# Weight pieces that hold four K tiles of both column tiles, a turned last K tile, and banks by last use, in a two-layer hybrid transformer

## The chip, the cores and the metric

The kernel runs on one core of one Trainium2 chip. The metric is the device time of one execution in microseconds. The kernel before takes 2865.7 us, the median of three runs (2864.64 to 2867.15).

## The reference

Two layers act on x, 256 tokens of width 2048, in float32. Each layer is a feed-forward half step, a mixer, and another feed-forward half step; each begins with an RMS norm and adds to x.

```python
for layer in range(DEPTH):
    x = x + 0.5 * swiglu(rms_norm(x, ffn1_norm[layer]), w1_gate, w1_up, w1_down)
    h = rms_norm(x, mix_norm[layer])
    x = x + (delta_pool_mixer(h, ...) if layer % 2 == 0 else mla_mixer(h, positions, ...))
    x = x + 0.5 * swiglu(rms_norm(x, ffn2_norm[layer]), w2_gate, w2_up, w2_down)
```

`swiglu` is `(silu(h @ w_gate) * (h @ w_up)) @ w_down` with 4096 hidden columns. Layer 0's mixer is a gated delta rule of 8 heads (convolution, chunked triangular solve) joined with a pooling over four window widths. Layer 1's is latent attention of 16 heads: two low-rank projections of width 512 with norms, up-projections, head norms, rotary angles, causal softmax. Nearly all arithmetic is the multiplication of 256 tokens by weights that are read once from HBM, about 508 MB.

## The kernel before

**Precision in two parts.** Every float32 operand is held as a high part (a rounded copy in the fast float32 format) and a low part (the remainder). For weights, `split` (lines 170 to 172) makes them on the chip: ScalarE casts a raw weight tile to `whi` (line 171), VectorE subtracts to `wlo` (line 172). For activations `split_hi_lo` does the same (lines 152 to 162), and the two parts lie side by side in one tile of 2 x 256 columns.

**A step.** `step` (line 207) multiplies one K tile of 128 rows for a pair of column tiles, each with a PSUM bank of its own. Two matmuls with the high weights take both parts of the activation (512 columns), then two with the low weights take the high part (256 columns). All go through `mm` (line 205), so the profile shows one line for them; tile names tell them apart (`mm<-xg,whi`). The two halves of a bank are added when the bank is read (`joined`, lines 231 to 235, or `add_residual`, lines 351 to 357).

**Weights.** `paired_weights` (line 190) takes two column tiles at a time. It loads 2048 columns (16 K tiles) of each with one DMA of 1 MB on SP's queue, into one of three raw buffers, and splits them in pieces of 1024 columns: 8 K tiles of tile A, 8 of tile B, and so on. `whi` and `wlo` have four buffers each. `pair` (line 217) takes one piece of A and one of B for every eight steps. A piece lies at a small offset in its buffer of 1088 columns: A's high part at 16 and low part at 0, B's at 0 and 16. In the latent attention's up-projections (`both_sides`, line 180) one raw piece of 1024 columns holds four K tiles of both column tiles, and is split in two halves of 512 at offsets of its own, with two operations on each engine.

**Phases.** A feed-forward block (`ffn`, line 368) goes through 32 pairs of a gate and an up tile with 16 K tiles each, then (`project`, line 359) 8 pairs of output tiles with 32 K tiles. After each pair of the latter VectorE adds the two tiles into x (line 355), and the next norm's inputs are made at once: `feed_parts` (ScalarE line 159, VectorE line 160) multiplies x by the norm's gain and splits it, `feed_squares` (GpSimd lines 330 and 336, at the end ScalarE and VectorE) sums the squares. The norm's scale itself is applied late: the first pair of the next phase runs on unscaled activations, and `end_norm` (line 342) then puts one product with a matrix of ones behind that pair's last matmul, takes the reciprocal root, and hands out R, by which every result is multiplied. In the very first block the first two pairs (`opening`, line 374) are interleaved with the loading of x. The mixers go the same way: projections of pairs, work of their own, and `project`.

**PSUM.** Eight banks: `banks` (line 140) gives each phase a ring for the pairs ("mm") and one for all else ("aux"), 6 and 2 in the feed-forward blocks, 4 and 4 in the mixers. Each ring begins with its lowest bank in every phase.

**Order.** The code is written in the order of issue per engine. Side work of the mixers (norms of heads, attention of a head, the solve) runs as generators (`Chains`, line 56): a clock counts the estimated matmul time of what has been issued, and `poll` continues a generator once the clock has passed what it yielded. `LAG` is 1500 ns of that clock. In the latent attention `latent` (line 867) squares a low-rank tile on ScalarE, with the squares' remainder on GpSimd (line 248), yields 2 LAG, and then issues the product that sums the squares; `head_norm` (line 887) does so for each head, also with 2 LAG.

## Time and profile before

| | |
|---|---|
| median of three runs | 2865.7 us |
| the profiled execution | 2850.95 us, its span 2848.9 us |
| TensorE, weight loads busy | 2823.4 us (99%), 2456.5 us (86%) |
| VectorE, ScalarE, GpSimd busy | 1844.6 (65%), 1434.2 (50%), 192.7 us (7%) |
| read from HBM | 507.74 MB, 179 GB/s over the span |
| mean granted TensorE clock | 0.999 of full speed |

PE is TensorE's matmuls, PEld its weight loads, DVE is VectorE, ACT ScalarE, POOL GpSimd, SP the engine that issues the weights' DMAs. Matmuls are pipelined: the record of one is longer than the time until the next one starts, so starts and counts say how fast the stream goes, and a share of 99% doesn't. By its stages the execution goes: opening to 35 us, first feed-forward block to 539, mixer of layer 0 to 952 with the next norm's first pair, second block to 1480, layer 1's first block to 2007, latent attention to 2318, last block to 2849. A wait is listed by the engine and line that waited, and what ended it.

### The profile page before, as it was taken

Reading aid. Unit: us, or ns where it says so; the run is one execution under the profiler, and the core shown is the slowest. Engines: PE = TensorE matmul, PEld = TensorE weight load, DVE = VectorE, ACT = ScalarE, POOL = GpSimd, SP = SyncE. Lnnn points to the kernel's source line nnn. Section 1 sums busy time; section 2 is a strip of 40 time slices with the busy share of each in tenths; the row PEclk is TensorE's granted clock in tenths of the full one; section 3 lists DMA queues with packets and bytes.
Section 4 is the critical chain, followed back from the end, with each engine's and each line's share of the span. In section 5 each row is a group of like instructions: output and inputs, shape, how many; then the busy total and the mean of one; then the engine's idle time right before and its main releaser. Section 6 shows DMA issues by size and latency. Waiting matters only on the chain.

```text
span 2848.9 us, 41026 instructions
## 1 busy us (share of the span) xinstructions
PE 2823.4 (99%) x16378; PEld 2456.5 (86%) x16378; DVE 1844.6 (65%) x2789; ACT 1434.2 (50%) x2251; POOL 192.7 (7%) x239
## 2 busy tenths in 40 slices
PE   9999999999999999999999999999999999999999
PEld 8888888888988888888888888888888888888888
DVE  7666656677787666565556666666688766666544
ACT  6454543475564444444444545443588444445433
POOL 1000002000003000000110000011122210000000
PEclk9999999999999999999999999999999999999999
DMA  6555555545235545445555455555433354554554
GB/s 230 202 189 196 195 190 182 184 152 183 84 146 194 190 180 201 181 186 190 187 185 200 188 196 194 191 187 197 169 111 121 134 195 177 194 190 178 201 197 148
DMA packets 78528, 512.62 MB, mean 180 GB/s; under 512 B 10880, under 2 KB 14720, under 8 KB 17536
## 3 DMA queue, kind: packets, MB, share of 16 engines
q1 hardware_dynamic: 74736, 506.76, 48.3%
q10 hardware_dynamic: 3600, 3.25, 0.3%
q8 instruction: 128, 2.10, 0.3%
q14 instruction: 64, 0.52, 0.1%
HBM read 507.74 MB, written 2.10 MB: 179 GB/s over the span
## 4 chain that ended last, share of the span: by engine, by line
PE 92%; DVE 4%; issue 3%; POOL 1%; ACT 0%; DMA 0%; SPq 0%; DVEq 0%; POOLq 0%; ACTq 0%
PE mm L205 88%; PE aux L205 4%; DVE wlo L172 2%; POOL sq L248 1%; DVE xg L160 1%; DMA x<-in_x 0%; DVE y L486 0%; PE aux L642 0%; ACT whi L171 0%; DVE x L355 0%; PE aux L974 0%; DVE cb L767 0%; PE aux L682 0%; PE aux L345 0%; DVE z L234 0%
## 5 line engine op out<-in xcount | busy, mean ns | idle before, releaser
L172 DVE TENSOR_TENSOR wlo<-raw,whi 128x1024 fp32r<-128x1024 f32 (+1 forms) x982 | 1204.0, 1231 | 781.3 <-ACT whi L171 779.4
L205 PE MATMUL mm<-xg,whi 128*128 128x512 f32 x4880 | 1533.8, 394 | 4.8 <-DVE x L355 3.5
L171 ACT CAST whi<-raw 128x1024 fp32r<-128x1024 f32 (+1 forms) x982 | 1003.4, 1032 | 1031.5 <-PE mm L205 717.7
L205 PEld LDWEIGHTS mm<-xg,wlo 128*128 128x128 f32 x4880 | 917.1, 188 | 205.3 <-DVE wlo L172 6.2
L205 PE MATMUL mm<-xg,wlo 128*128 128x256 f32 x4880 | 973.9, 278 | 3.6 <-DVE wlo L172 3.5
L205 PEld LDWEIGHTS mm<-xg,whi 128*128 128x128 f32 x4880 | 745.8, 188 | 12.6 <-ACT whi L171 6.5
L205 PE MATMUL mm<-g,whi 128*128 128x512 f32 x2048 | 636.6, 392 | 0.0
L205 PEld LDWEIGHTS mm<-g,wlo 128*128 128x128 f32 x2048 | 384.5, 188 | 92.5 <-DVE wlo L172 7.5
L205 PE MATMUL mm<-g,wlo 128*128 128x256 f32 x2048 | 406.8, 278 | 2.0 <-DVE wlo L172 0.4
L205 PEld LDWEIGHTS mm<-g,whi 128*128 128x128 f32 x2048 | 309.8, 188 | 0.0
L156 ACT CAST g<-u 128x256 fp32r<-128x256 f32 x128 | 52.0, 406 | 166.4 <-DVE u L410 166.1
L135 ACT ACTIVATE t<-t 128x256 f32<-128x256 f32 x128 | 53.4, 417 | 100.0 <-DVE t L235 100.0
L157 DVE TENSOR_TENSOR g<-u,g 128x256 fp32r<-128x256 f32 x128 | 54.4, 425 | 57.5 <-ACT g L156 57.5
L330 POOL TENSOR_TENSOR acc<-x 128x256 f32<-128x256 f32 x6 | 3.7, 616 | 1193.8 <-DVE x L355 1146.6
L355 DVE SCALAR_TENSOR_TENSOR x<-mm,x 128x256 f32<-128x256 f32 x128 | 45.4, 417 | 57.9 <-PE mm L205 57.9
L330 POOL TENSOR_TENSOR sq<-x 128x256 f32<-128x256 f32 x70 | 54.0, 771 | 426.2 <-DVE x L355 332.7
L205 PE MATMUL mm<-o,whi 128*128 128x512 f32 x256 | 81.4, 395 | 0.0
L336 POOL TENSOR_TENSOR acc<-acc,sq 128x256 f32<-128x256 f32 x70 | 80.0, 1143 | 5.3
L234 DVE TENSOR_TENSOR t<-mm,t 128x256 f32<-128x256 f32 x177 | 72.7, 416 | 8.9 <-ACT t L233 8.6
L160 DVE SCALAR_TENSOR_TENSOR xg<-x,gains,xg 128x256 fp32r<-128x256 f32 x96 | 73.5, 802 | 5.1 <-ACT xg L159 5.1
L233 ACT COPY t<-mm 128x256 f32<-128x256 f32 x177 | 64.6, 372 | 8.4 <-PE mm L205 8.3
L205 PEld LDWEIGHTS mm<-o,wlo 128*128 128x128 f32 x256 | 47.9, 188 | 14.6 <-DVE wlo L172 5.5
(258 smaller groups left out, 1816.5 us busy)
## 6 DMA issues: line engine op xcount, KB each, us to landing
raw<-in_w1d SPq DMA_DIRECT2D x64, 1024.0 KB, 5.1
raw<-in_w2g SPq DMA_DIRECT2D x64, 1024.0 KB, 4.9
raw<-in_w2u SPq DMA_DIRECT2D x64, 1024.0 KB, 4.8
raw<-in_w2d SPq DMA_DIRECT2D x64, 1024.0 KB, 5.1
raw<-in_w1g SPq DMA_DIRECT2D x62, 1024.0 KB, 4.9
raw<-in_w1u SPq DMA_DIRECT2D x62, 1024.0 KB, 4.8
raw<-in_wqk SPq DMA_DIRECT2D x16, 1024.0 KB, 4.8
raw<-in_wgo SPq DMA_DIRECT2D x16, 1024.0 KB, 4.8
```

Source lines behind the costliest of these rows:

```text
L135: a = nc.scalar.activation(out, in_, func, **kw)
L156: nc.scalar.copy(dst[:, 0, :], src)
L157: nc.vector.tensor_tensor(dst[:, 1, :], src, dst[:, 0, :].bitcast(F32), op=ALU.subtract)
L160: nc.vector.scalar_tensor_tensor(dst[:, 1, :], src, scale, dst[:, 0, :].bitcast(F32), op0=ALU.mult, op1=ALU.subtract)
L171: self.last_cast = self.nc.scalar.copy(hi, src)
L172: self.nc.vector.tensor_tensor(lo, src, hi.bitcast(F32), op=ALU.subtract)
L205: return self.nc.tensor.matmul(out, lhsT, rhs, start=start, stop=stop)
L233: self.nc.scalar.copy(out, ps[:, S : 2 * S])
L234: self.nc.vector.tensor_tensor(out, ps[:, 0:S], out, op=ALU.add)
L330: eng.tensor_tensor(dst, self.x[d], self.x[d], op=ALU.mult)
L336: eng.tensor_tensor(self.acc, self.acc, dst, op=ALU.add)
L355: self.nc.vector.scalar_tensor_tensor(x, ps[:, c], 0.5, x, op0=ALU.mult, op1=ALU.add)
```

## The change

- `paired_weights` takes a list in which two column tiles have been interleaved on the host (`couples`): 512 columns (four K tiles) of one, then 512 of the other. One raw tile of 2048 columns then holds 8 K tiles of both. `both` splits 1024 columns with one operation per engine into both tiles' pieces of four K tiles, which lie 528 columns apart in the buffer. The second column tile comes first in a couple, so the high matmuls load from offset 528 and then from 0. The low matmuls of a step now go in reversed order, 0 and then 528.
- Gate and up, the down projections, both mixers' input and output projections and the up-projections use it. The latent attention's one unpaired input tile has a function of its own, `lone`. In the opening, each of the two loads of a block holds both tiles of one pair, not one tile of two pairs.
- Of the last K tile before a norm's product, the low matmuls come before the high ones (`turn`).
- `banks` sorts each ring by last use, longest unused first.
- In `latent` the wait before the squares' product is 4 LAG, not 2; in `head_norm` it is 3 LAG, not 2.

```diff
     def banks(self, mm, aux):
-        self.bank = {"mm": list(range(mm)), "aux": list(range(8 - aux, 8))}
+        recent = self.recent
+        self.bank = {"mm": sorted(range(mm), key=recent.index), "aux": sorted(range(8 - aux, 8), key=recent.index)}
     def psum(self, tag):
         q = self.bank[tag]
         q.append(q.pop(0))
+        self.recent.remove(q[-1])
+        self.recent.append(q[-1])
...
-    def both_sides(self, raw, h):
...
+    def couple(self, t):
+        return t[:, 0 : 2 * APART].rearrange("p (u c) -> p u c", u=2)[:, :, 0:512]
+    def both(self, raw, h):
+        hi, lo = (self.couple(t) for t in self.weight_tiles())
+        self.split(hi, lo, raw[:, h : h + 1024].rearrange("p (u c) -> p u c", u=2))
+        return [(hi[:, u, :], lo[:, u, :]) for u in (1, 0)]
     def paired_weights(self, slabs):
-        for u in range(0, len(slabs), 2):
-            two = slabs[u : u + 2]
-            for c in range(0, two[0].shape[1], 2048):
-                raws = [self.raw_tile() for _ in two]
-                for raw, ap in zip(raws, two):
-                    self.nc.sync.dma_start(raw, ap[:, c : c + 2048])
+        for ap in slabs:
+            for c in range(0, ap.shape[1], 2048):
+                raw = self.raw_tile()
+                self.nc.sync.dma_start(raw, ap[:, c : c + 2048])
                 for h in (0, 1024):
-                    yield [self.piece(raw, h, side) for raw, side in zip(raws, (SIDE_A, SIDE_B))]
+                    yield self.both(raw, h)
...
-    def step(self, ps, ws, act, first, last):
+    def step(self, ps, ws, act, first, last, turn=False):
         whole = act.rearrange("p a t -> p (a t)")
-        for o, (hi, lo) in zip(ps, ws):
-            self.mm(o, hi, whole, start=first, stop=False)
-        for o, (hi, lo) in zip(ps, ws):
-            self.last_mm = self.mm(o[:, 0:S], lo, act[:, 0, :], start=False, stop=last)
+        def high():
+            for o, (hi, lo) in zip(ps, ws):
+                self.last_mm = self.mm(o, hi, whole, start=first, stop=last and turn)
+        def low():
+            for o, (hi, lo) in list(zip(ps, ws))[::-1]:
+                self.last_mm = self.mm(o[:, 0:S], lo, act[:, 0, :], start=False, stop=last and not turn)
+        for f in ((low, high) if turn else (high, low)):
+            f()
...
-    def pair(self, stream, acts):
+    def pair(self, stream, acts, turn=False):
         K = len(acts)
-        ps = None
-        for k0 in range(0, K, 8):
-            pieces = next(stream)
-            ps = ps or [self.psum("mm") for _ in pieces]
-            for k in range(k0, k0 + 8):
-                c = slice((k - k0) * P, (k - k0 + 1) * P)
-                self.ch.wait(lambda: acts[k] is not None)
-                self.step(ps, [(hi[:, c], lo[:, c]) for hi, lo in pieces], acts[k], k == 0, k == K - 1)
-                self.ch.poll()
+        ps = [self.psum("mm") for _ in range(2)]
+        for k in range(K):
+            if k % 4 == 0:
+                pieces = next(stream)
+            c = slice(k % 4 * P, k % 4 * P + P)
+            self.ch.wait(lambda: acts[k] is not None)
+            last = k == K - 1
+            self.step(ps, [(hi[:, c], lo[:, c]) for hi, lo in pieces], acts[k], k == 0, last, turn and last)
+            self.ch.poll()
         return ps
...
             lat.setdefault(tag, []).append(o)
-            yield 2 * LAG
+            yield 4 * LAG
...
             b.squares(sq, t)
-            yield 2 * LAG
+            yield 3 * LAG
...
+def couples(u):
+    n, _, K = u.shape
+    return u.reshape(n // 2, 2, P, K // 512, 512)[:, ::-1].transpose(0, 2, 3, 1, 4).reshape(n // 2, P, 2 * K)
```

## Rows read from the trace of the kernel before

**Rows 1.** The page, busy time: engine, us, share of the span, instructions.
```profile
PE 2823.4 (99%) x16378; PEld 2456.5 (86%) x16378; DVE 1844.6 (65%) x2789; ACT 1434.2 (50%) x2251; POOL 192.7 (7%) x239
```
**Rows 2.** Windows, line 205: start:end, us, busy (matmuls), granted clock, DMA, GB/s.
```profile
1000.00:1100.00 100.00, 100.00 (x574) 87.09 (x573) 1.00 0.50 190
...
1600.00:1700.00 100.00, 100.00 (x591) 88.59 (x590) 1.00 0.49 190
```
**Rows 3.** Windows of three gate-and-up phases: PE, PEld, DVE, ACT, POOL busy (instructions).
```profile
952.00:1337.00 385.00, 385.00 (x2200) 335.42 (x2200) 237.89 (x341) 188.51 (x272) 2.96 (x3) 1.00 0.50 187
...
1480.00:1865.00 385.00, 385.00 (x2265) 340.90 (x2264) 243.93 (x349) 189.86 (x279) 2.97 (x3) 1.00 0.51 192
...
2318.00:2703.00 385.00, 385.00 (x2200) 335.46 (x2200) 235.81 (x339) 186.42 (x269) 0.00 (x0) 1.00 0.50 187
```
**Rows 4.** Timeline of PE at a pair start of a down projection: start, length.
```profile
431.56 0.62 PE L205 MATMUL mm<-g,whi 128*128 128x512 f32 x2
432.02 0.80 PE L205 MATMUL mm<-g,wlo 128*128 128x256 f32 x2
432.65 0.62 PE L205 MATMUL mm<-g,whi 128*128 128x512 f32 x2
```
**Rows 5.** Timeline of DVE just before the same pair start.
```profile
427.55 1.53 DVE L172 TENSOR_TENSOR wlo<-raw,whi 128x1024 fp32r<-128x1024 f32 x1
429.00 1.70 DVE L160 SCALAR_TENSOR_TENSOR xg<-x,gains,xg 128x256 fp32r<-128x256 f32 x2
430.62 1.75 DVE L172 TENSOR_TENSOR wlo<-raw,whi 128x1024 fp32r<-128x1024 f32 x1
```
**Rows 6.** Waits of PEld, four stretches in order: us in total, times, longest.
```profile
PEld mm L205 <- DVE wlo L172: 2.6, 6, 0.5
...
PEld mm L205 <- DVE wlo L172: 4.8, 12, 1.1
...
PEld mm L205 <- DVE wlo L172: 2.3, 6, 0.5
...
PEld mm L205 <- DVE wlo L172: 6.5, 13, 0.9
```
**Rows 7.** Groups by form, 2060 to 2200: busy us, mean ns, idle before.
```profile
L172 DVE TENSOR_TENSOR wlo<-raw,whi 128x512 fp32r<-128x512 f32 x40 | 30.1, 760 | 5.1 <-ACT whi L171 5.0
...
L172 DVE TENSOR_TENSOR wlo<-raw,whi 128x1024 fp32r<-128x1024 f32 x11 | 14.6, 1325 | 2.0 <-ACT whi L171 2.0
```
**Rows 8.** Waits of PE, whole execution: us in total, times, longest.
```profile
PE mm L205 <- DVE x L355: 3.5, 3, 1.2
```
**Rows 9.** Chain that ended last, around 1479 us: start, length, what.
```profile
1478.47 1.10 DVE x L355 x3
...
1479.71 3.48 PE mm L205 x18
```
**Rows 10.** Timeline of PE in the latent attention.
```profile
2028.55 0.38 PE L205 MATMUL aux<-sq,ones_r 128*128 128x256 f32 x1 [3.57 <-POOL sq L248]
```
**Rows 11.** Timeline of POOL there, two operations merged.
```profile
2024.38 4.99 POOL L248 TENSOR_TENSOR sq<-sqf,sq 128x256 fp32r<-128x256 f32 x2 [35.78 <-ACT sq L247]
```
**Rows 12.** Timeline of DVE there: first and last of eight pairs.
```profile
2023.80 0.49 DVE L851 TENSOR_SCALAR rs<-rs 128x256 f32<-128x256 f32 x2
...
2027.43 0.48 DVE L858 TENSOR_SCALAR trig<-trig 128x256 f32<-128x256 f32 x2
```
**Rows 13.** Window behind that wait, columns as in rows 3; clock third from last.
```profile
2029.10:2032.50 3.40, 3.40 (x13) 2.96 (x12) 1.69 (x2) 0.00 (x0) 0.28 (x1) 0.50 0.19 34
```
**Rows 14.** Timeline of PE where all matmuls go to one bank.
```profile
2033.92 0.40 PE L205 MATMUL mm<-xg,whi 128*128 128x512 f32 x1
...
2034.62 0.39 PE L205 MATMUL mm<-xg,whi 128*128 128x512 f32 x1
```
**Rows 15.** The page, costliest groups: busy us, mean ns, idle before.
```profile
L205 PE MATMUL mm<-xg,whi 128*128 128x512 f32 x4880 | 1533.8, 394 | 4.8 <-DVE x L355 3.5
...
L205 PE MATMUL mm<-g,whi 128*128 128x512 f32 x2048 | 636.6, 392 | 0.0
```

More of the change, by code (lines that the diff above doesn't have):

```diff
@@ L26 @@
 EXTRA = 64
-SIDE_A = (16, 0)
-SIDE_B = (0, 16)
-SIDE_V = (48, 48)
+APART = 528
+SINGLE = (16, 0)
+VALUES = (48, 48)
 GH = 8
@@ L113, in __init__ @@
         self.n = 0
+        self.recent = list(range(8))
         self.ch = Chains()
@@ L172, in split, with piece @@
         self.nc.vector.tensor_tensor(lo, src, hi.bitcast(F32), op=ALU.subtract)
-    def piece(self, raw, h, side=SIDE_A):
+    def piece(self, raw, h, side):
         hi, lo = (t[:, c : c + 1024] for t, c in zip(self.weight_tiles(), side))
@@ L359, in project @@
     def project(self, slabs, acts, half, after):
-        st = self.paired_weights([slabs[d] for d in range(KT)])
+        st = self.paired_weights([slabs[d] for d in range(KT // 2)])
         for d in range(0, KT, 2):
@@ L365, in project, with ffn @@
                 after(d + e)
-    def ffn(self, wg, wu, wd, after, start=False):
+    def ffn(self, wgu, wd, after, start=False):
         nc, tc = self.nc, self.tc
@@ L391, in opening @@
                         ws = []
-                        for w, side in enumerate((SIDE_A, SIDE_B)):
-                            hi, lo = (part(t, o) for t, o in zip(tiles[w], side))
-                            self.split(hi, lo, part(raw, 1024 * w))
-                            ws.append((hi, lo))
+                        for f in range(2):
+                            hi, lo = (self.couple(t)[:, :, cols] for t in tiles[f])
+                            self.split(hi, lo, quad(raw[:, 1024 * f : 1024 * f + 1024]))
+                            ws.append([(hi[:, u, :], lo[:, u, :]) for u in (1, 0)])
                         for m in range(n):
                             d = 4 * c + k0 + m
+                            w = slice(P * m, P * m + P)
                             for f in range(2):
-                                cols = slice(P * m, P * m + P)
-                                self.step(ps[f], [(hi[:, f, cols], lo[:, f, cols]) for hi, lo in ws], xg[d], d == 0, d == KT - 1)
+                                last = d == KT - 1
+                                self.step(ps[f], [(hi[:, w], lo[:, w]) for hi, lo in ws[f]], xg[d], d == 0, last, last and f == 1)
                 self.load_rest()
@@ L415, in ffn @@
             early = opening() if start else []
-            st = self.paired_weights([w[f] for f in range(len(early), NF) for w in (wg, wu)])
+            st = self.paired_weights([wgu[f] for f in range(len(early), NF)])
             g, R = [], None
@@ L465, in gdn @@
         xg = b.xg
-        st = b.paired_weights([i["wqk"][u] for u in range(2 * GH)] + [i["wz"][u] for u in range(GH)]
-                              + [i["wv"][u] for u in range(GH)] + [i["wu"][u] for u in range(GH)])
+        st = b.paired_weights([i["wgi"][u] for u in range(20)])
         R = None
@@ L471, in units @@
             nonlocal R
-            ps = b.pair(st, xg)
+            ps = b.pair(st, xg, R is None)
             if R is None:
@@ L736, in wpool @@
             for h in (0, 1024):
-                yield b.piece(raw, h)
+                yield b.piece(raw, h, SINGLE)
         pw = wpool()
@@ L823, in mla @@
         xg = b.xg
-        st = b.paired_weights([i["wmi"][u] for u in range(9)])
+        st = b.paired_weights([i["wmi"][u] for u in range(4)])
         R = None
@@ L916, in mla @@
         kp = tl([P, S], "kp")
-        kpc = ch.spawn(head_norm(units()[0], 64, khp, kp, True), delay=LAG)
+        kpc = ch.spawn(head_norm(scaled(b.lone(i["wmk"], xg), R), 64, khp, kp, True), delay=LAG)
         o = [None] * MH
@@ L928, in chunks @@
                     for h, kind in enumerate(kinds):
-                        yield b.piece(raw, 1024 * h, SIDE_V) if kind == "v" else b.both_sides(raw, 1024 * h)
+                        yield b.piece(raw, 1024 * h, VALUES) if kind == "v" else b.both(raw, 1024 * h)
         cks = chunks()
```

68 lines of the change are left out of this document (35 added, 33 removed).

## The prediction

> **What bounds the kernel now.** I read the page first. TensorE is busy 2823.4 of 2848.9 us [rows 1], so the change can pay only where TensorE waits or where its matmuls come more slowly than they could. VectorE (1844.6) and ScalarE (1434.2) have room on average, and matter only where one of their results ends a wait. Then I went by stretches, because a busy TensorE is not one at its peak. A *step* here is four matmuls: one K tile of a pair, two high ones of 512 columns and two low ones of 256. In the hundred microseconds from 1600 there start 591 matmuls, from 1000 only 574, both at 100.00 busy and a granted clock of 1.00 (the 2.4 GHz level) [rows 2]. So a step takes 4 x 100 / 591 = 0.677 us at one level and 4 x 100 / 574 = 0.697 at the other: two levels 3% apart under the same clock and the same code. Gate-and-up phases of equal work show it whole: 2200 matmuls in 385 us in layer 0's and layer 1's second feed-forward block, 2265 in layer 1's first [rows 3]. The same count in shorter windows gives the slower level from 880 to 1375, from 2310 to the end and in most of the mixer of layer 0 (560 to 830), some 1300 us with what lies between.
>
> The waits come third. In a down projection the high pair of a new pair of column tiles starts at 431.56, its low pair at 432.02, and the next high pair only at 432.65 [rows 4]. At a step of 0.677, with 0.46 from the high pair to the low pair, the low pair should take 0.22 and takes 0.63: 0.41 lost at one pair start. VectorE tells why: one weight remainder at 427.55, then two activation parts at 429.00, and the remainder of the second column tile only at 430.62, ending at 432.37 [rows 5]. A step needs the remainders of both column tiles, and the second stands behind VectorE's work for the previous pair. The list of waits gives what these cost the weight loads, by stretch: 2.6 us from 35 to 550, 4.8 from 550 to 952, 2.3 from 952 to 1491, 6.5 from 2019 to 2318 [rows 6]; the stretch 1491 to 2019 has the same 2.6 as the first.
>
> **Part 1: pieces of four K tiles of both column tiles.** Splits, bytes and matmuls stay the same in number, with one exception below. Before, splits A and B are both needed at the first step of eight; now the first is needed there and the second four steps = 2.7 us later. Two buffers come free together before; now the first of the two comes free 2.7 us earlier. Every split is thus due no earlier, and can start no later, which is why I exclude a loss here. In the down projections the remainder of 427.55 alone then feeds the first four steps (to 431.56 + 2.7 = 434.3), and the second, ending at 432.37, has 1.9 us to spare. So the three rows of down projections go whole: 2.6 + 2.3 + 2.6 = 7.5 us. In the two mixers (4.8 + 6.5 = 11.3) VectorE is late for other reasons too; the excess is mostly one split long, so I take 8 of them. That is 15.5 us, with 7.5 and 7.5 + 11.3 = 18.8 as ends. Next late at a pair start is the cast of the first piece, which ScalarE makes well ahead.
>
> The exception is the multi-head up-projection, where a unit's split was two half operations on each engine and becomes one. VectorE's halves take 760 ns each against 1325 for a whole one in that stretch [rows 7]: 0.2 us less for each of 20 units, on an engine that isn't the bound. I cost it at nothing (ends: 0 and 20 x 0.2 = 4 us). The strided output of a split has no row of its own; as it is two runs of 512 elements, its price lies between one whole (1325) and two halves (1520), and 0.2 us more on a split due 2.7 us apart is hidden. The DMAs keep their size, 1 MB from SP; each is now needed alone instead of in twos, so none is due earlier. In the opening the two loads of a block change from gate and up to first and second pair; the remainders of both are still needed within one step, so I leave it at zero.
>
> **Part 2: order of the banks.** Three times TensorE waits 1.2 us on line 355, the residual update [rows 8]. The chain shows one: 1.10 us of three updates, then the first matmul of the next phase [rows 9]. A feed-forward block hands out 80 banks of a ring of six, so its last pair sits in banks 0 and 1, and the next phase starts with bank 0 again. With the longest unused first, it takes 2 and 3. The activations of the last two tiles are needed only 14 steps = 9.5 us later, so nothing is late next: 3.5 us, ends 0 and 3.5 (the weights at the new phase's start might be late instead).
>
> **Part 3: later polls in the latent attention.** At 2028.55 a product waits 3.57 us for GpSimd's square remainder [rows 10]. GpSimd's two operations hold it from 2024.38 for 4.99 us [rows 11], beside a run of eight pairs on VectorE from 2023.80 to 2027.9, the rotary angles [rows 12]. Then the granted clock is 0.50 (the 1.2 GHz level) for 3.4 us [rows 13], after TensorE had started nothing for that wait: half of 3.4 = 1.7 us more. The chain's wait of 2 LAG becomes 4 LAG, so the product is queued 3 us later. The release stays where it is (about 2028.5), the product arrives about 2027.6, and a wait of about 0.9 is left, 0.5 more for the second square. I take 3.6 + 1.7 - 1.4 = 3.9, ends 0 and 5.3. What queues behind that product is every later matmul; a wait that short leaves the clock alone, I assume. The head norms' extra LAG moves their products too; they may lengthen the last heads' chain by 1.5 us before the output projection's last K tiles. I set that against what other GpSimd waits lose, at zero (ends -1.5 and +1.5).
>
> *One rule of the Trainium skill stands against part 3's release time.* GpSimd's first operation took most of the 4.99 us of [rows 11], far longer than any single VectorE operation of [rows 12] (the pairs take 0.48 to 0.75). "SBUF — State Buffer", section "Who interferes with whom", says that of two contending operations the loser is blocked until the other one finishes. By that, GpSimd would get in after one VectorE operation, its result would be there before 2027.6, no wait would be left, and part 3 would be worth 5.3. The row shows it held through the run, so I go by the row.
>
> **Part 4: the turned last K tile.** Six norms; the same four matmuls in another order. The product's weight load then lies beside a matmul of 512 columns instead of 256. At most the difference between a high matmul (0.23) and a low one (0.11) is hidden at each, 6 x 0.12 = 0.7 us; I take 0, ends 0 and 0.7.
>
> **Sum.** 15.5 + 3.5 + 3.9 = 22.9 us, with ends 7.5 - 1.5 = 6 and 18.8 + 4 + 3.5 + 5.3 + 1.5 + 0.7 = 33.8. The profiled execution took 2850.95 by itself; 2850.95 - 22.9 = 2828.1. The timed runs have a median of 2865.7, 14.75 more. That is as much as 14.75 / 0.03 = 490 us more at the slower level would give, which I can't show. I put the sum on the median: **2843 us**, its own range 2832 to 2860.
>
> **The rivals.** All of them turn on the two levels, which nothing in the diff names. Both last for hundreds of microseconds without a wait, and in the trace they change where TensorE had waited, for instance at the pair starts; the waits that go are therefore also what moved the stream from one level to the other.
> *(a) The slower level stays.* If the mixer of layer 0 leaves the stream at the slower level, as from 952 [rows 3], no pair start moves it back. The faster stretches from about 1375 to 2010, some 630 us, are then at the slower level: 630 x 0.03 = +19. That gives 2865.7 - 23 + 19 = 2862. For it: two of four gate-and-up phases are slow as a whole. Against: a mixer has many other waits.
> *(b) The faster level stays.* The slow stretches from 880 to 1375 and from 2310 to the end, some 1030 us, become fast: -30, that is 2813. For it: the last pair starts before either stretch have such a wait. Against: slow phases also follow a norm's product without one.
> *(c) The low matmuls in reversed order cost time.* Each step now ends on the bank that the next one starts with, and its middle two share a bank. Where all matmuls of the trace run in one bank, a high and a low take (2034.62 - 2033.92) / 2 = 0.35 [rows 14], 0.70 for four: no worse than the slower level, but no better. If one bank is the reason, all of (4880 + 2048) / 2 = 3464 steps [rows 15] lie at 0.697; some 1300 us, 1300 / 0.697 = 1870 steps, are slow already, so 1590 others pay 0.02 us each, 32 us. Net +9: 2875, slower than before. It decides from 22.9 / 3464 = 6.6 ns a step on. Against it: those matmuls also load from one side of both weight tiles in turn, so the bank is not shown as the cause.
> *(d) The change does less than it says.* Only the down projections' waits go, 7.5 us: 2858.
>
> **How the numbers follow.** My case 0.38, (a) 0.24, (b) 0.22, (c) 0.09, (d) 0.07. A difference of 0.2% (5.7 us) is about what a measurement of this kernel can tell from no change. Mine and (b) are faster (0.60, less 0.01); of (a), at 2862, half is faster, 0.10 within and 0.02 slower; (d) is mostly faster (0.05, 0.02 within); of (c) 0.07 is slower and 0.02 within. Together 0.76 faster, 0.15 within, 0.09 slower. The range leaves out the far side of (b) and most of (c): 2808 to 2869.
>
> **What would show it.** Right: no remainder among the waits at pair starts of the down projections; no wait on line 355 at the three phase starts; no 0.50 clock after 2029 and a wait of about 1 us there. The counts of matmuls in windows of 100 us tell the rivals: 574 through layer 1's first feed-forward block means (a), 591 in both second feed-forward blocks (b), 574 or fewer everywhere (c). The prediction is wrong if weight waits move to the middle of a pair, or if a third level appears.

## The result and the profile after

The changed kernel takes **2794.27 us** (median of 4 runs, 2793.86 to 2794.64), the kernel before 2865.17 (4 runs, 2855.18 to 2867.15): a ratio of 0.9759, 95% interval 0.9737 to 0.9782. It is 70.9 us faster; 22.9 were forecast, and 2794 lies below the range. Of the two profiled executions, which the views below belong to, before took 2850.95 and after 2794.64: 56.3 us. The other 14.6 are a difference between executions of the kernel before; an experiment below shows where they lie.

The page of after (engine, us, share of the span, instructions) answers to [rows 1]: PE is busy for nearly the whole span, 43.3 us less in all, with the same 16378 matmuls.
```profile
PE 2780.1 (100%) x16378; PEld 2445.0 (88%) x16378; DVE 1848.9 (66%) x2769; ACT 1439.7 (52%) x2231; POOL 225.4 (8%) x239
```
The first thing that the prediction wanted looked at is the level. Windows of after (start:end, us, PE busy and matmuls, PEld busy and loads, granted clock, DMA share, GB/s), line 207, which is line 205 of before: 590 or 591 in both, where [rows 2] had 574 and 591.
```profile
1000.00:1100.00 100.00, 100.00 (x591) 88.58 (x590) 1.00 0.57 193
1600.00:1700.00 100.00, 100.00 (x590) 88.51 (x589) 1.00 0.57 191
...
945.00:1330.00 385.00, 385.00 (x2265) 340.78 (x2266) 1.00 0.57 192
1467.70:1852.70 385.00, 385.00 (x2265) 340.99 (x2266) 1.00 0.57 193
2277.00:2662.00 385.00, 385.00 (x2264) 341.31 (x2265) 1.00 0.58 194
```
The last three answer to [rows 3]: where 2200, 2265 and 2200 matmuls started in 385 us, now 2264 or 2265 do in every phase. That is the faster level in each.

Then the waits. The list of waits of after (us in total, times, longest) has one wait for a weight remainder left, in the opening (2.6), against 21.9 us in 45 waits over the whole of before, whose four rows are [rows 6] and their like. No wait on the residual update (line 376, before 355) is in it, against [rows 8]; GpSimd's square remainder is waited for 0.7 us in two waits, against 3.57 in the one of [rows 10].
```profile
PEld mm L207 <- DVE wlo L176: 2.6, 1, 2.6
PE aux L207 <- POOL sq L269: 0.7, 2, 0.4
```
At a pair start of a down projection (the timeline of PE: start, length) high and low pairs now follow each other evenly, 0.45 and 0.23 us apart; in [rows 4] the low pair at the pair start took 0.63.
```profile
425.49 0.62 PE L207 MATMUL mm<-g,whi 128*128 128x512 f32 x2
425.94 0.39 PE L207 MATMUL mm<-g,wlo 128*128 128x256 f32 x2
426.17 0.62 PE L207 MATMUL mm<-g,whi 128*128 128x512 f32 x2
```

To see where the 56 us lie I cut the execution at the products of the six norms, numbered 1 to 6 in order of time, whose starts the timeline gives (line 345 before, 366 after), and at the start of the last matmul. (The span goes 4.4 us beyond that.) The column "after, no turn" is an experiment told below: the kernel after without the turned tile. Stretches in us:

| stretch, from product to product | before | after, no turn | after |
|---|---|---|---|
| start to product 1 | 34.90 | 36.88 | 36.95 |
| layer 0, first feed-forward block | 515.00 | 508.90 | 508.91 |
| layer 0, mixer | 401.93 | 398.68 | 398.76 |
| layer 0, second feed-forward block | 538.91 | **538.03** | **522.70** |
| layer 1, first feed-forward block | 527.63 | **538.02** | **522.71** |
| layer 1, mixer (latent attention) | 299.44 | 286.89 | 286.70 |
| layer 1, second feed-forward block | 526.71 | 511.69 | 511.69 |

The two columns of after differ in two rows alone (bold), by 15.3 us each: one block of 523 us, 3% of it. The turn is the step from "after, no turn" to "after", 2823.5 - 2792.8 = 30.7 us of span. All else is the step from "before" to "after, no turn", 2848.9 - 2823.5 = 25.4, and that step is not waits alone. In two of its rows a whole block changes its level: layer 1's first block, fast in before, is slow without the turn (10.4 us longer, in spite of the waits that went), and layer 1's second block, slow in before, is fast without any turn (15.0 shorter). The two nearly cancel. So against the kernel before the faster level is gained in the two second feed-forward blocks (16.2 and 15.0 us with what waits there were), and the turn keeps layer 1's first block from losing it.

### The profile page after: what moved, and what is told of

Same layout as the page of the kernel before. It is cut to its first block, busy times and chain, and to the rows that moved or that the text cites. A ratio compares the mean times of both kernels' runs of the same rounds, so it can differ in the third digit from the quotient of the medians.

```text
span 2792.8 us, 41323 instructions
## 1 busy us (share of the span) xinstructions
PE 2780.1 (100%) x16378; PEld 2445.0 (88%) x16378; DVE 1848.9 (66%) x2769; ACT 1439.7 (52%) x2231; POOL 225.4 (8%) x239
## 4 chain that ended last, share of the span: by engine, by line
PE 96%; DVE 2%; issue 1%; ACT 1%; POOL 0%; DMA 0%; DVEq 0%; ACTq 0%; POOLq 0%
PE mm L207 91%; PE aux L207 4%; DVE wlo L176 1%; POOL sq L269 0%; PE aux L663 0%; POOL osq L269 0%; DVE t L256 0%; DMA gains<-in_gains 0%; ACT whi L175 0%; PE aux L992 0%; DVE t L255 0%; DVE xg L164 0%; ACT rs L136 0%; PE aux L366 0%; DVE cb L788 0%
## 5 line engine op out<-in xcount | busy, mean ns | idle before, releaser
L207 PE MATMUL mm<-xg,whi 128*128 128x512 f32 x4880 | 1516.8, 392 | 0.0
L207 PE MATMUL mm<-xg,wlo 128*128 128x256 f32 x4880 | 955.8, 277 | 2.2 <-DVE wlo L176 2.2
L207 PE MATMUL mm<-g,wlo 128*128 128x256 f32 x2048 | 399.3, 276 | 0.0
L351 POOL TENSOR_TENSOR sq<-x 128x256 f32<-128x256 f32 x70 | 75.2, 1090 | 1560.1 <-DVE x L376 1442.3
L269 POOL TENSOR_TENSOR sq<-sqf,sq 128x256 fp32r<-128x256 f32 x49 | 48.5, 998 | 157.2 <-ACT sq L268 129.3
L256 DVE TENSOR_TENSOR t<-t,R 128x256 f32<-128x256 f32 x137 | 56.8, 417 | 0.1
```

The costliest lines, as they stand in the source:

```text
L207: return self.nc.tensor.matmul(out, lhsT, rhs, start=start, stop=stop)
L256: self.nc.vector.tensor_tensor(out, out, R, op=ALU.mult)
L269: nc.gpsimd.tensor_tensor(dst[:, 1, :], sq, dst[:, 0, :].bitcast(F32), op=ALU.subtract)
L351: eng.tensor_tensor(dst, self.x[d], self.x[d], op=ALU.mult)
```

## The experiments

Each had the kernel before run on the same chip; its median there was between 2846 and 2866, so the kernels are set beside each other by what their profiles show in the same windows. T stands for the theory that the turned tile sets the level, W for the rival that it follows where TensorE last waited. Levels are given as the time of a step, 0.68 us (590 matmuls in 100 us) or 0.70 (573 or 574).

**The kernel before, once more** (no edit).

> The kernel before, unchanged, to see another execution of it. If the two levels of a step (about 590 matmuls in 100 us, or about 574) decide its time, an execution near 2865 us has some 490 us more at 574 than the one of 2850.95 us, for instance in layer 1's first feed-forward block (1480 to 2000); one near 2851 us has the same stretches as before. If the 14 us lie outside the span, the counts are the same at any time.

2864.18 us. Windows of this execution (columns as in the page: start:end, us, PE busy and matmuls, clock, DMA share, GB/s):
```profile
100.00:200.00 100.00, 100.00 (x574) 1.00 0.49 186
1000.00:1100.00 100.00, 100.00 (x574) 1.00 0.50 190
1700.00:1800.00 100.00, 100.00 (x590) 1.00 0.51 190
```
The profiled execution of before had 590 in the first window and 574 and 590 in the others, as here. From product 1 to product 2 this one took 526.6 us instead of 515.0, and to product 1 36.85 instead of 34.90. So the 13 us between two executions of one kernel are the first feed-forward block at one level or the other, and 2 us in the opening. After has 590 in that block: this is probably most of the 14.6 us between the two ways of comparing, though the slower timed runs of before have no trace that shows it.

**The turn alone: taken from after, added to before.**
```diff
# after without the turn
-        for f in ((low, high) if turn else (high, low)):
+        for f in (high, low):
# before + turn: step(..., turn) as in after, low order not reversed, for the last K tile ahead of each norm's product
+            self.step(..., k == 0, k == K - 1, turn and k == K - 1)
```


> The changed kernel with the last K tile before a norm's product in the usual order (high, then low). Theory 'turn': the turned tile is what puts the stream on the faster level at each norm's product; without it the slow stretch that begins in layer 0's output projection (842) lasts beyond the norm's product at 945, to 2000: 1050 us at 3%, about 2825 us or more. Theory 'no waits': the level stays where it is when nothing is waited for, and the turn does nothing: within 3 us of 2794, but then the step from slow to fast at 945 needs another cause. Theory 'order of the low matmuls': 2794.

> The kernel before with the turned last K tile alone. Theory 'turn': every gate-and-up phase has about 590 matmuls in 100 us; the two slow ones gain 11 us each and the projections behind them some, 2825 to 2845. Theories 'no waits' and 'order of the low matmuls': no change from before within its scatter (2850 to 2867).

Without the turn 2825.01 us (2824.38 to 2825.74; ratio to before 0.9902, 0.9870 to 0.9934). Before with the turn 2828.39 (2821.68 to 2835.13, three runs near 2822 and three near 2834, of which the slowest is the profiled one; 0.9916, 0.9888 to 0.9944). Windows of after without the turn:
```profile
860.00:940.00 80.00, 80.00 (x458) 1.00 0.58 196
1000.00:1100.00 100.00, 100.00 (x573) 1.00 0.56 188
...
2400.00:2500.00 100.00, 100.00 (x590) 1.00 0.58 196
```
and of before with it:
```profile
100.00:200.00 100.00, 100.00 (x573) 1.00 0.49 187
1000.00:1100.00 100.00, 100.00 (x590) 1.00 0.51 193
...
2400.00:2500.00 100.00, 100.00 (x590) 1.00 0.52 199
```
The first kernel has none of the waits at pair starts and is at 573 through two blocks. Its stream enters product 3 at the slower level (458 matmuls in the 80 us from 860) and keeps it; that of after enters it at the slower level too (459) and leaves it at the faster. No wait stands in either, so the turn makes that switch. In the second kernel 590 behind products 3 and 4 says nothing, since its stream comes to both at 0.68 already (963.12 - 962.44 at product 3). Into product 6 it comes at 0.70, and it goes on at the faster level (590 from 2400), with the waits all in place:
```profile
2315.10 0.63 PE L205 MATMUL mm<-xg,whi 128*128 128x512 f32 x2
...
2315.80 0.63 PE L205 MATMUL mm<-xg,whi 128*128 128x512 f32 x2
...
2317.20 0.59 PE L351 MATMUL aux<-acc,ca 128*128 128x256 f32 x2
```
The kernel before comes to product 6 at 0.70 and stays there (2200 in 385 us, [rows 3]). So W fails at a norm's product. It does not fail everywhere: in the down projections of before a wait at a pair start does move the level. Near 1373 us, at one such wait, the stream goes from 136 matmuls in 24 us to 119 in 20, 0.71 to 0.67 for four.

The switch can be seen at the matmul in the timelines of PE around product 3, of after
```profile
944.16 0.62 PE L207 MATMUL mm<-xg,whi 128*128 128x512 f32 x2
944.62 0.59 PE L366 MATMUL aux<-acc,ca 128*128 128x256 f32 x2
944.86 0.81 PE L207 MATMUL mm<-xg,whi 128*128 128x512 f32 x2
...
945.75 0.62 PE L207 MATMUL mm<-xg,whi 128*128 128x512 f32 x2
...
946.43 0.39 PE L207 MATMUL mm<-xg,whi 128*128 128x512 f32 x1
```
and of after without the turn:
```profile
944.23 0.40 PE L207 MATMUL mm<-xg,wlo 128*128 128x256 f32 x2
944.46 0.60 PE L366 MATMUL aux<-acc,ca 128*128 128x256 f32 x2
...
945.59 0.62 PE L207 MATMUL mm<-xg,whi 128*128 128x512 f32 x2
...
946.29 0.63 PE L207 MATMUL mm<-xg,whi 128*128 128x512 f32 x2
```
The step that starts at 945.75 in after takes 0.68 (to 946.43); the one at 945.59 without the turn 0.70 (to 946.29), and each stays so through two blocks, a thousand microseconds.

**The order of the low matmuls, and where the low weights lie.** Rival (c) of the prediction, tried in both kernels.
```diff
# bank order not reversed, low weights 16 elements further on
-            for o, (hi, lo) in list(zip(ps, ws))[::-1]:
+            for o, (hi, lo) in zip(ps, ws):
-        hi, lo = (self.couple(t) for t in self.weight_tiles())
+        hi, lo = (self.couple(t, at) for t, at in zip(self.weight_tiles(), (0, 16)))
# bank order not reversed, offsets kept: the two halves of a low tile change places (remainder in two operations)
+            self.nc.vector.tensor_tensor(lo[:, 1 - u, :], src[:, u, :], hi[:, u, :].bitcast(F32), op=ALU.subtract)
# before with the reversed order, offsets kept
-SIDE_A = (16, 0)
-SIDE_B = (0, 16)
+SIDE_A = (16, 16)
+SIDE_B = (0, 0)
```


> The changed kernel with the low matmuls in the old order of banks (A, B, A, B), the low halves moved by 16 columns so that the sequence of weight offsets (16, 0, 0, 16 modulo 32) stays. Theory 'order of the low matmuls' (two neighbours in one bank make the faster level): slow stretches return, 2810 to 2835. Theories 'turn' and 'no waits': 2794, counts of 590 everywhere in the feed-forward blocks.

> The changed kernel with the low matmuls in the old order of banks (A, B, A, B) and the low halves exchanged within their buffer, so that the offsets of the weights, taken modulo 64 elements, stay 16, 0, 0, 16 as in the changed kernel (after_abab had 16, 0, 32, 16). The remainder is made by two half operations. Theory 'offset': the third level of after_abab came from the 32; this one is back at 590 in the feed-forward blocks, 2794 to 2802. Theory 'bank order': the alternation of banks made it; again about 573 everywhere, 2855.

> The kernel before with the low matmuls in reversed order alone (banks A, B, B, A); the offsets of the low halves are exchanged so that the sequence of offsets stays 16, 0, 0, 16. Theory 'bank order': the faster level holds from the opening on, below 2830. Theory 'offset and turn': as the kernel before, 2838 to 2866, with its slow stretches where chance puts them.

With the offset changed 2857.71 us (2855.91 to 2860.28; 1.0018, 0.9998 to 1.0038); with the offsets kept 2806.69 (2806.52 to 2809.04; 0.9818, 0.9793 to 0.9842); before with the reversed order 2854.12 (2831.15 to 2857.98; 0.9974, 0.9952 to 0.9997). One window of each of the first two:
```profile
1000.00:1100.00 100.00, 100.00 (x574) 1.00 0.57 187
```
```profile
1000.00:1100.00 100.00, 100.00 (x590) 1.00 0.60 197
```
The order of the banks does nothing that these runs can tell: without it 590 stands behind products 3, 4 and 6 (only the first feed-forward block is slow, 573 at 100, about the 12 us that are missing), and with it before keeps its pattern, 573 at 1000, 590 at 1700, 573 at 2400. That is against (c). What the first kernel changed besides, the low weights 16 elements further on, goes with 573 or 574 in all windows read in the feed-forward blocks, behind turned tiles with their products too. It was not run without the turn, and its twin with the offsets kept makes the remainder in two operations, so the offset is the likely cause and not isolated.

**More turned tiles.**
```diff
-            self.step(..., acts[k], k == 0, last, turn and last)
+            self.step(..., acts[k], k == 0, last, last)          # last K tile of every pair
+            self.step(..., acts[k], k == 0, last, k % 2 == 1)    # every second K tile
```


> The changed kernel with the last K tile of every pair turned, not only ahead of a norm's product. If the turned tile by itself moves the stream to the faster level, the slow stretches of the output projections and of the mixers (about 465 us in the changed kernel) shrink: up to 465 x 0.03 = 14 us, 2780 to 2790. If it is the norm's product behind the turned tile that moves it, 2794 within 4 us.

> The changed kernel with every second K tile turned, so that low matmuls stand in fours and high ones in fours. If a run of low matmuls is what moves the stream, the faster level holds everywhere: 2775 to 2790. If four weight loads in a row behind matmuls of 256 columns cannot be hidden, each second step pays: by the low pair's 0.46 us at the slower level against 0.45, up to 30 us more, 2825.

2855.57 (2853.26 to 2857.54; 0.9976, 0.9963 to 0.9990) and 2857.07 (2854.56 to 2859.73; 0.9982, 0.9966 to 0.9998): both lose the 60 us again. With every second K tile turned the stream is slow throughout, 572 to 574 from 100, 1000, 1700 and 2400, also behind the six products. The timeline of PE in the first kernel, at the next turned tile behind product 3 (957.97), which has no product behind it:
```profile
968.40 0.63 PE L207 MATMUL mm<-xg,wlo 128*128 128x256 f32 x4
968.86 1.09 PE L207 MATMUL mm<-xg,whi 128*128 128x512 f32 x4
...
970.03 0.63 PE L207 MATMUL mm<-xg,whi 128*128 128x512 f32 x2
...
970.73 0.63 PE L207 MATMUL mm<-xg,whi 128*128 128x512 f32 x2
```
Steps of 0.70 from here on (970.03 to 970.73); from product 3 to this pair they had been 0.68, and so it goes behind each product. A turned tile without a product takes the stream from the faster level to the slower.

**The product elsewhere.** If tile and product together set the level, they should do so in the output projections too, which have none.
```diff
+            reset = not half and d == 0          # in the second kernel also: and self.gain < 3 (layer 0 only)
+            pss = self.pair(st, acts, reset)
+            if reset:
+                none = self.psum("aux")
+                self.behind(self.nc.tensor.matmul(none[:, :S], self.ones, self.x[KT - 1], start=True, stop=True), self.last_mm)
```


> The kernel after, with one thing added in both output projections: the last K tile of the first pair is turned, and a product of the same kind as the norm's (fp32, 128 x 128 by 256) is put right behind it; its result is not used. In the kernel after the output projection of layer 0 runs at 573 matmuls in 100 us from 842.4 until the norm's product at 945.75. Theory T (a turned tile with an fp32 product behind it puts the stream at the faster level, wherever it stands): from about 853.5 on the count is 590, so (945.75 - 853.5) x 0.03 = 2.8 us less, and two products of 0.43 us more; the output projection of layer 1 is at the faster level already. 2794.3 - 2.8 + 0.9 = 2792.4. Rival W (the levels follow where TensorE last waited; the turned tile only happens to stand there): 573 stays to 945.75, 2794.3 + 0.9 = 2795.2.

> The kernel after, with a turned last K tile and an unused fp32 product behind the first pair of the output projection of layer 0 only. With it in both output projections the window from 860 to 940 rose from 459 to 473 matmuls, while that of layer 1 (2180 to 2270) fell from 525 to 512, because there the product was followed by a low pair. Theory H: 473 in the first window, and about 525 in the second if its stream is left as in the kernel after: 2794.3 - 2.7 + 0.4 = 2792.0; 2794.7 if layer 1's output projection comes out slow for another reason, as it did with the old banks and the old polls. Rival: the first window goes back to 459, 2794.7.

2793.74 us (2793.69 to 2794.65) and 2793.23 (2790.74 to 2793.95). Windows of the two output projections, of after and then of the kernel with the product in both:
```profile
860.00:940.00 80.00, 80.00 (x459) 1.00 0.59 196
2180.00:2270.00 90.00, 90.00 (x525) 1.00 0.50 168
```
```profile
860.00:940.00 80.00, 80.00 (x473) 1.00 0.59 194
2180.00:2270.00 90.00, 90.00 (x512) 1.00 0.52 169
```
In layer 0 it works as T says, 459 to 473. In layer 1 it fails: the stream is slow there. The timeline of PE shows that the order of issue had put a low pair behind that product and not the next tile's high pair. With the product in layer 0 alone the windows hold 473 and 526. Its median is 1 us below that of after, and the 0.2% that can be told from no change would be 5.7: no better version that I can claim.

**The other parts.** After with the old banks, after with the old polls, and before with everything but the pieces.
```diff
# old banks
+        self.bank = {"mm": list(range(mm)), "aux": list(range(8 - aux, 8))}
# old polls
-            yield 4 * LAG
+            yield 2 * LAG
...
-            yield 3 * LAG
+            yield 2 * LAG
# before with turn, banks and polls: no new pieces, low order not reversed
```


> The kernel after with the banks handed out from number 0 at each phase, as before. Theory T (turn sets the level, each wait is a term by itself): three waits of 1.2 us on the residual update come back, the counts of matmuls in 100 us stay at 590 in all gate-and-up phases and down projections: 2794.3 + 3.5 = 2797.8. Rival W (waits set the level): the stream falls to 573 behind the three phase starts until the first pair's norm product or further; one such phase of 1100 us would cost 33 us: 2810 or more.

> The kernel after with the polls of the latent attention as before (2 LAG in both places). Theory T: the wait of about 3.6 us for GpSimd's square remainder comes back near 2000 us, and with it some 3.4 us at a granted clock of 0.50; the levels elsewhere stay: 2794.3 + 3.9 to 5.3 = 2798.2 to 2799.6. Rival W: the wait also leaves the stream at the slower level through the mixer to the norm's product at its end, some 290 us x 0.03 = 9 us more: 2807.

> The kernel after without its new pieces: the kernel before with the turned tile, the order of the banks and the later polls. Theory T: before + turn took 2828.4; less 3.5 for the banks and 3.9 for the polls: 2821. The new pieces are then worth 2821 - 2794 = 27: some 15.5 of weight waits, and some 12 of the first gate-and-up phase, which before + turn ran at the slower level from 100 to 424; counts of 590 behind every norm's product after that. Rival W: the weight waits at the pair starts, which are back, send the stream to the slower level within the down projections and at the phases behind them: 2840 to 2860.

2799.44 us (2798.34 to 2801.78), 2799.76 (2797.25 to 2803.47) and 2826.79 (2817.06 to 2830.04; 0.9928, 0.9900 to 0.9957). The waits of each, in that order:
```profile
PE mm L207 <- DVE x L376: 3.5, 3, 1.2
```
```profile
PE aux L207 <- POOL sq L269: 3.8, 7, 1.7
```
```profile
PEld mm L209 <- DVE wlo L176: 22.0, 43, 2.5
```
All three keep 589 to 591 in the gate-and-up phases behind products 3, 4 and 6: waits come back, levels stay. The old banks cost 5.2 us, of which the three waits are 3.5 and layer 1's output projection at the slower level (514 matmuls from 2180 to 2270 instead of 525) about 1.9. The old polls cost 5.5, with the same 1.9 in it (513), so the part itself is worth about 3.6 by the medians. That is rough: the five runs lie between 2797 and 2803, and in the profiled one, the slowest, layer 1's mixer takes 295.05 us, 8.35 more than in after. Its longest wait for the square remainder is 1.7 us, and behind it, from 2002 to 2004, the granted clock is 0.50. Without the pieces the 22.0 us of weight waits are there and the first feed-forward block is slow (573 in the window from 100); between them they make up the 32.5 us to after, some 15 by the level and the rest by the pieces.

**What decides at the product.** Five of the six norms in three more kernels (the opening keeps its turned tile): the product between the high and the low pair of the last K tile; the last K tile not turned but the first of the next pair (its low products are overwritten, a small part of the result that is left out); no turn, and the product issued twice.
```diff
# middle: high, product, low
+            if f is low and middle:
+                m = self.nc.tensor.matmul(self.norm_ps[:, :S], self.ones, self.acc, start=True, stop=True)
# low pairs on both sides
+            self.step(..., k == 0, last, k == 0 and self.lead)
# twice
+            m2 = self.nc.tensor.matmul(ps[:, :S], self.ones, self.acc, start=True, stop=True)
+            self.behind(m2, m)
```


> The kernel after with no turned tile at five of the six norms (the opening keeps its own); the norm's product is put between the high pair and the low pair of that last K tile: high, product, low, and then the next tile's high pair. In the kernel after it is high, product, high. Theory H (a high pair has to stand on both sides of the product): the stream comes out at the slower level behind each of the five products, as in the output projection of layer 1 with the added product: 573 in 100 us at 1000 and at 1700, about as without the turn or slower, 2825 to 2857. Rival K (a high pair ahead of the product is enough): 590 at both, 2794.

> The kernel after with the last K tile not turned at five of the six norms, and the first K tile of the next pair turned instead: low, product, low, high. (The low products of that one K tile are overwritten by its high ones, so a small part of the result is left out.) Theory H (a high pair on both sides): 573 in 100 us behind the products, 2825 to 2857. Rival L (the same kind on both sides, whichever): 590 behind them, 2794.

> The kernel after without the turned tile at five of the six norms, and the norm's product issued twice there: low, product, product, high. Theory H (the kinds of the matmuls on both sides decide): 573 behind the products as without the turn, 2825 + 5 x 0.43 = 2827. Rival S (only the time or the number of products between two steps decides, and the turn shifts it): 590 behind some or all of them, 2794 to 2815.

2840.57 us (2838.28 to 2844.25; 0.9971, 0.9949 to 0.9993), 2825.00 (2792.52 to 2843.03; 0.9913, 0.9883 to 0.9943) and **2795.54** (2795.28 to 2795.74; 0.9824, 0.9784 to 0.9864). Theory H (the kinds of matmul on both sides of the product decide) falls with the last one: no tile is turned at these five norms, and the level is the faster. The timeline of PE around its product 3, a slow stream (0.70 from 942.80 to 943.50) that leaves it at 0.68:
```profile
942.80 0.40 PE L208 MATMUL mm<-xg,wlo 128*128 128x256 f32 x2
...
943.50 0.40 PE L208 MATMUL mm<-xg,wlo 128*128 128x256 f32 x2
943.74 0.60 PE L367 MATMUL aux<-acc,ca 128*128 128x256 f32 x2
944.17 0.59 PE L370 MATMUL aux<-acc,ca 128*128 128x256 f32 x2
944.42 0.81 PE L208 MATMUL mm<-xg,whi 128*128 128x512 f32 x2
945.07 0.39 PE L208 MATMUL mm<-xg,wlo 128*128 128x256 f32 x2
...
945.75 0.39 PE L208 MATMUL mm<-xg,wlo 128*128 128x256 f32 x2
```
and around product 6 of the kernel with the product in the middle, a fast stream (0.68 from 2304.73 to 2305.41) that leaves it at 0.70:
```profile
2304.73 0.61 PE L207 MATMUL mm<-xg,whi 128*128 128x512 f32 x2
...
2305.41 0.62 PE L207 MATMUL mm<-xg,whi 128*128 128x512 f32 x2
2305.87 0.59 PE L227 MATMUL aux<-acc,ca 128*128 128x256 f32 x2
2306.11 0.59 PE L207 MATMUL mm<-xg,wlo 128*128 128x256 f32 x2
2306.53 0.63 PE L207 MATMUL mm<-xg,whi 128*128 128x512 f32 x2
...
2307.23 0.63 PE L207 MATMUL mm<-xg,whi 128*128 128x512 f32 x2
```
So the runs give a table and no reason. It holds for products 3 to 6, with the weights' offsets of after and steps that are not turned elsewhere. *Faster whatever came in:* turned tile with the product behind it and a high pair next; two products in a row (one case that came in slow, product 3). *Slower whatever came in:* a turned tile alone; the product between high and low pair (one case that came in fast, product 6). *As it came in:* one product behind an unturned tile (without the turn, 573 stays 573 at product 3 and 590 stays 590 at product 6). The kernel with low pairs on both sides did the same in its profile (573 at 1000, 590 at 2400), and one of its ten runs, 2792.5, took as long as a run that is fast throughout. With the low weights moved, or with every second K tile turned, the first entry fails: the stream stays slow behind each of these products. In the gate-and-up phases between the products neither level gives way to the other until something else is put in.

Product 1 is another case, as the opening interleaves two pairs. In after without the turn the product starts at 36.88, between the two matmuls of one high pair (36.65 and 37.13): the stream comes in at 0.70 and goes on at 0.68, without a turned tile. So it does in every kernel of these runs with the product in that place and after's offsets and steps. In the kernels where a low matmul comes right behind product 1 (the old pieces, and the one with the halves changed about) the first block is slow, but for the profiled execution of before.

## Why the prediction was wrong

**The step that failed is part 4.** I took the turned last K tile at 0, with ends of 0 and 0.7 us, because the same four matmuls come in another order. Undone alone it was worth 30.7 us of span (2823.5 to 2792.8), in the two bold rows of the table. The price of a level was right (3%), and in rival (b) the length that it applied to; wrong was the sentence that nothing in the diff names the levels, and with it a sum that left them where they were. The diff changes the order of instructions right ahead of each phase of [rows 3], and I priced that order by what a weight load can hide, the one cost for which I had a row. With no row for a turned tile, 0 and 0.7 were no bounds: the ends had to hold one phase at either level.

**Rival (b) had the size, and half of the reason at most.** The faster level in both second feed-forward blocks, priced at 30 us, came as (b) said, and 22.9 + 30 from the profiled execution's 2850.95 is 2798, 3.4 above what was measured. But it held the removed waits to be what kept the stream fast. In layer 0's second block they don't: after without the turn has no such waits and is at 573 there. In layer 1's second block the same kernel is at 590 without a turn, and before with the turn at 590 with all the waits, so either way leads there. What brings the stream to product 6 at the faster level is open: in after and in the kernel without the turn it comes so, with the old banks or the old polls it comes at the slower one, and the turn mends it.

**Where the sum was put.** I took it from the median instead of the profiled execution, and so kept 14.75 us in the forecast that I could not explain. They go with the first feed-forward block at the slower level, as the repeated run of before shows it (2864.18), and after, at 590 there in its profile, does not have them. Why the first block of before can come out either way was not settled. That of after came out fast in its profile and stayed within 0.8 us in the timed runs; its turned tile is not the reason, since after without any turn has 590 there as well and before with a turn 573. It goes with the place of product 1 between two high matmuls, which came with the new pieces in all kernels but the one with the halves changed about.

**The waits went as forecast.** Part 1: taken 15.5, ends 7.5 and 18.8; the four waiting rows and their like went entirely, 21.9 to 2.6 us, and the 2.6 left are in the opening. Its worth by itself is an estimate: the 33.5 us of span between after and the kernel without the pieces, less the 15.3 of one block's level, some 18. Part 2: 3.5, all of it, as the old banks give back. Part 3: taken 3.9, measured about 3.6, roughly as said above. The latent attention's product waits twice 0.36 us, where I expected 0.9 and 0.5; by [rows 10] TensorE stood at that product from 2024.98, and 3 us later is 2027.98 and not 2027.6, so the first should have been 0.5; the clock of 0.50 of [rows 13] is gone (1.00 from 2000.8 to 2006). The opening, set at zero, took 36.95 us to product 1 and 34.90 in before; but the repeated run of before took 36.85, and the kernels with the opening of after lie between 34.79 and 37.36, so these 2 us belong to the execution and not to the change.

In sum, before and after without the turn lie 25.4 us of span apart, 27.4 without the 2 us of the openings, where I said 22.9 for the waits. Each has the slower level in most of two feed-forward blocks, before in the two second ones, after without the turn in layer 0's second and layer 1's first. So the levels nearly cancel in this difference, and the waits are about what is left.

**GpSimd beside VectorE.** GpSimd's two operations in the timeline of POOL, of after:
```profile
1997.64 3.12 POOL L269 TENSOR_TENSOR sq<-sqf,sq 128x256 fp32r<-128x256 f32 x2 [33.85 <-ACT sq L268]
```
They took 3.12 us here and 4.99 in [rows 11]. VectorE's unbroken rotary run ends at 1999.2 here, 1.6 us after they began; in before at 2027.9, 3.5 us after. Both times they last 1.5 us longer than the run beside them, twice the 0.73 us that the shortest of these operations takes in either trace, which goes with the reading that they are held while it lasts. The rule of the Trainium skill ("SBUF — State Buffer", section "Who interferes with whom") that the loser waits for the other's one operation would, read as the prediction read it, have let them in within the 0.3 to 0.4 us of one such operation; the row does not agree.

**The other rivals.** (a), a slower level that stays: did not come, though after without the turn is such a kernel for two blocks. (c): the order of the banks cost nothing that the runs can tell. (d): all weight waits behind the opening went, not only those of the down projections.

## What to carry to other kernels

When equal work under one clock runs at two speeds, find the last odd instruction ahead of the switch, and treat every edit to the order around it as one with the whole stretch at stake: price it at both levels, not at the nanoseconds that the edit itself moves. Before a change is judged by such a kernel's time, count matmuls per window in the executions of both, or a level that came by chance is taken for its effect. Where a part is one line, undo it alone and look at the table by stretches, and at the level at which each stretch was entered: a fast stretch that was fast when it came in says nothing of what stands at its start.

## What the runs showed of the hardware that was not expected

- A stream of one repeated step of four matmuls has two steady speeds at a granted clock of 1.00, 0.677 and 0.697 us, for up to a thousand microseconds; one fp32 product of 0.43 us more or less at one place selected which (product 3 of the kernel with two, 590 against 573 at 1000).
- Turning a K tile has the opposite effect with and without the fp32 product behind it (0.70 to 0.68 at 945.75, 0.68 to 0.70 at 970.03).
- Where the low weights start in their tile goes with the speed: 16 elements further on, and no window read in a feed-forward block held more than 574, at 2857.7 us against 2806.7 with the offsets kept.
- A wait of 1.7 us for GpSimd was followed by a granted clock of 0.50 from 2002 to 2004 (after with the old polls); two waits of 0.36 us at the same place were not (1.00 from 2000.8 to 2006 in after).
- What makes the two speeds, in the chip, these runs do not show.
